# Modulation vectors as columns and a scaled transposing product in the opening stage of a hybrid attention and DeltaNet layer

## The chip, the cores and the metric

The kernel runs on one core of one Trainium2 chip. The core has five engines with queues of their own: TensorE (PE, with its weight loads shown apart as PEld), VectorE (DVE), ScalarE (ACT), GpSimd (POOL) and SyncE (SP, which here issues the loads). The metric is the device time of one execution in microseconds. The median of three runs of the kernel before is 1299.49 us (1299.34 to 1300.92).

## What is computed

One layer of a diffusion backbone over 512 latent tokens and 256 context tokens, with 1024 channels, in float32. Cut to what matters here:

```python
mod_lat = jax.nn.silu(c) @ w_mod + b_mod          # 1024 -> 6 x 1024
mod_ctx = jax.nn.silu(c_ctx) @ w_mod + b_mod
sh1, sc1, g1, sh2, sc2, g2 = split(mod_lat, 6)
hx = rms_norm(x)   * (1 + sc1)  + sh1             # latent rows
hc = rms_norm(ctx) * (1 + csc1) + csh1            # context rows
...                                               # hx, hc @ w_in, attention, gated DeltaNet, merge
x = x + g1 * merged
x = x + g2 * conv_ffn(rms_norm(x) * (1 + sc2) + sh2)
return rms_norm(x, final_norm_w)
```

The opening stage computes the first two of the six vectors for both `c` and `c_ctx` (2048 columns of `w_mod`), the RMS norms, and `hx` and `hc`, transposed so that channels lie on the 128 partitions. The other four vectors are made later, beside other work.

## The kernel before

The text below calls by their letters the steps that the string `ORD` lists. PE's instructions are kept in the order of that list (`pinned`, L548); on the other engines a scheduler orders instructions by priority and by its own estimate of time.

- **Loads** (`LORD`, L422 to L455): SP issues `x0 x1 x2` (the context rows and two halves of the latent rows, 1 MB each, tiles `xs`), `w0` to `w7` (eight chunks of `w_mod`, 1 MB each, tiles `wm`, `WB` = 3 buffers), and `h0 h1` (the first two weight tiles of the projections, `wraw`, 2 buffers), kept in this order. Then come the rope tables `tabs` and `wrow`.
- **d**: 16 products on zeros at the start (`warm`, L551).
- **Row norms** (L464 to L470): ACT squares each 128-row tile and sums the squares, DVE and POOL (the power of -0.5) make the factor `rs`, DVE multiplies the rows `xs` by it.
- **x** (`x_cols`, L507): four transposes of 128x128 of the scaled rows into one of two banks `pt`, copied out by DVE (even steps) or ACT (odd steps).
- **g** (`gemv`, L474): one of four blocks of 512 modulation columns. The moving operand is the chunk of `w_mod`, 512 wide, and the stationary one the columns of silu(c) and silu(c_ctx). For the first 4 or 6 of the 8 row blocks k (`FKS`) the weights are split into a rounded part `wmh` (ACT) and a rest `wml` (DVE or POOL, `GN`), both float32r, and `cs4` holds the split vectors; the other k go as plain float32. The result `pm` is a row, copied to `mrow` by DVE.
- **m** (`mod_cols`, L494): four small transposes of `mrow` into columns, and four additions on DVE.
- **y** (`modulate`, L519): for one pair of channel blocks, scale and shift (latent rows on DVE, context rows on POOL), then the split into a rounded part (ACT, `hxH`, `hcH`) and a rest (DVE, `hxL`, `hcL`).
- **p** (`early_proj`, L538): the products of one channel block with the two first weight tiles (`hw`), 12 matmuls, into the banks `pc` and `mb`. p0 and p1 need y0, p2 and p3 need y1, and so on.

After the opening follow the projections of keys, values and queries (tile `pq`, weights `w_aq`), whose matmuls are also kept in program order, with the other modulation vectors woven in (tiles `wmd`, `macc`).

Of the kernel before, what the change touches and what calls it, by code (L numbers as in the profile page):

```python
# [14 lines left out]
P = 128  # L15
D = 1024
# [19 lines left out]
KV = 10  # L36
GN = '023'
FKS = '4466'
ORD = 'd4 x0 x1 x2 x3 x4 x5 x6 x7 g0 x8 x9 x10 x11 m0 y0 g1 m1 y1 p0 g2 p1 m2 y2 p2 g3 p3 m3 p4 y3 p5 p6 p7'
RK = 1.0  # L40
# [3 lines left out]
TG = 1  # L44
WHB = 3
PMB = 1
XV, YV = 0, 2
NS = 2
# [6 lines left out]
LPIN = 1  # L55
LORD = 'x0 x1 x2 w0 w1 w2 w3 h0 h1 w4 w5 w6 w7'
WB = 3
P0 = 1
# [20 lines left out]
def hybrid_layer_body(tc, x, ctxt, xT, consts, cols, rows, w_mod1, w_mod2, w_db, w_aq, w_cm, w_pa, w_pd, w_out,  # L79
                      w_up, w_down, outT, dbg=None):  # L80
    nc = tc.nc
    V, A, G, SP = nc.vector, nc.scalar, nc.gpsimd, nc.sync
    pinned = [False]

# [22 lines left out]
    def tt(out, a, b, op, eng=None):  # L107
        (eng or V).tensor_tensor(out=out, in0=a, in1=b, op=op)  # L108

    def ts(out, a, s1, op0, s2=None, op1=None, eng=None):  # L110
        if op1 is None:
            (eng or V).tensor_scalar(out=out, in0=a, scalar1=s1, scalar2=None, op0=op0)
        else:
            (eng or V).tensor_scalar(out=out, in0=a, scalar1=s1, scalar2=s2, op0=op0, op1=op1)  # L114

# [3 lines left out]
    def act(out, a, f=AF.Copy, **kw):  # L119
        A.activation(out, a, f, **kw)  # L120

# [12 lines left out]
    with es:  # L134
# [7 lines left out]
        def first():  # L142
            return tc.high_priority(offset=2000000)
# [276 lines left out]
        with m1_es:  # L420
# [5 lines left out]
            def ordered_load(out, in_):  # L426
                i = SP.dma_start(out, in_)
                if LPIN:
                    tc.keep_in_program_order(i)

            hw = []
            for op in LORD.split():
                i = int(op[1])
                with sooner():
                    if op[0] == "w":
                        wms.append(m1.tile([P, 4, 512], F32, name="wm", tag="wm", bufs=WB))
                        ordered_load(wms[i], w_mod1[i // 2, i % 2])
                    elif op[0] == "h":
                        h, part = order[i]
                        raw = ws.tile([P, 1024], F32, name="wraw", tag="wraw", bufs=2)  # L440
                        ordered_load(raw, w_cm[8 * part + h])
                    elif i == 0:
                        ordered_load(xs[0], ctxt)
                    else:
                        ordered_load(xs[i], x[:, 2 * i - 2:2 * i, :])
                if op[0] == "h":
                    with first():
                        hi, lo = (m1.tile([P, 1024], F32R, name=n, tag=n, bufs=NS) for n in ("whi", "wlo"))
                        split(hi, lo, raw)
                        hw.append((hi, lo))  # L450
            with sooner():
# [7 lines left out]
            V.tensor_copy(csl, cs.rearrange("p (k two) -> p k two", two=2)[:, :, 0])  # L459
            cs4 = m1.tile([P, KT, 4], F32R, name="cs4")  # L460
            split(cs4[:, :, 0:2], cs4[:, :, 2:4], cs.rearrange("p (k two) -> p k two", two=2))
            ss = m1.tile([P, 6], F32, name="ss")
            rs = m1.tile([P, 6], F32, name="rs")
            for i in range(3):  # L464
                for t in range(2):
                    act(hxH[:, 6:8, :].rearrange("p a b -> p (a b)"), xs[i][:, t, :], AF.Square, accum_out=ss[:, 2 * i + t:2 * i + t + 1])
                sl = slice(2 * i, 2 * i + 2)
                rsqrt(rs[:, sl], ss[:, sl], 1.0 / D, EPS)
                for t in range(2):
                    ts(xs[i][:, t, :], xs[i][:, t, :], rs[:, 2 * i + t:2 * i + t + 1], ALU.mult)  # L470
            m2 = lambda t, o: t[:, o:o + 16].rearrange("p (s k) -> p s k", s=2)
            wsl = lambda k: slice(k * P, k * P + P)

            def gemv(nb, k0=0, k1=KT):  # L474
                if k0 == 0:
                    mpm[nb] = mps.tile([P, 512], F32, name="pm", tag="pm", bufs=PMB)[0:4]
                ps = mpm[nb]
                for k in range(k0, k1):
                    wm, j = wms[2 * nb + k // 4], k % 2
                    if k >= int(FKS[nb]):  # L480
                        mm(ps[0:2], cs[:, 2 * k:2 * k + 2], wm[:, k % 4, :], False, k == KT - 1)
                        continue
                    if j == 0:
                        wmh = m1.tile([P, 2, 512], F32R, name="wmh", tag="wmh", bufs=WHB)
                        wml = m1.tile([P, 2, 512], F32R, name="wml", tag="wml", bufs=WHB)
                        act(wmh, wm[:, k % 4:k % 4 + 2, :])
                        tt(wml, wm[:, k % 4:k % 4 + 2, :], wmh, ALU.subtract, G if k % 4 == 0 and str(nb) in GN else V)
                    mm(ps, cs4[:, k, :], wmh[:, j, :], k == 0, False)
                    mm(ps[0:2], cs4[:, k, 0:2], wml[:, j, :], False, k == KT - 1)
                if k1 == KT:  # L490
                    mrows[nb] = m1.tile([4, 512], F32, name="mrow", tag="mrow", bufs=2)
                    V.tensor_copy(mrows[nb], ps)

            def mod_cols(nb, mrow):  # L494
                pst = xbank()[:, 0, 0:16].rearrange("p (a b) -> p a b", b=4)
                for i in range(4):
                    T.transpose(pst[:, i, :], mrow[:, i * P:(i + 1) * P], ident[0:4, 0:4])
                ks = slice(2 * nb, 2 * nb + 2)
                p4 = pst.rearrange("p (s k) r -> p s k r", s=2)
                for j, md in enumerate((mod, modc)):  # L500
                    tt(m2(md, 0)[:, :, ks], p4[:, :, :, j], m2(col, S_BMOD)[:, :, ks], ALU.add)
                    tt(m2(md, 0)[:, :, ks], p4[:, :, :, 2 + j], m2(md, 0)[:, :, ks], ALU.add)

# [3 lines left out]
            def x_cols(j):  # L507
                i, kp = j // 4, j % 4
                dst = stash[1][kp] if i == 0 else stash[0][kp][:, :, 256 * i - 256:256 * i]
                pt = mps.tile([P, 2, 256], F32, name="pt", tag="pt", bufs=NB - PMB - NS)  # L510
                for a in range(2):
                    for t in range(2):
                        transpose(pt[:, a, t * P:(t + 1) * P], xs[i][:, t, wsl(2 * kp + a)])
                if j % 2 or j < XV:
                    act(dst, pt)
                else:
                    V.tensor_copy(dst, pt)

            def modulate(kp):  # L519
                for (hh, hl, md, pair), st in zip(sides, stash):  # L520
                    n = hh.shape[2]
                    hfs = []
                    for a in range(2):
                        k = 2 * kp + a
                        hf = m1.tile([P, n], F32, name="hf", tag="hf%d" % n, bufs=HB)
                        if n == NL or YV:
                            ts(hf, st[kp][:, a, :], md[:, 8 + k:9 + k], ALU.mult, md[:, k:k + 1], ALU.add,
                               G if YV == 2 and n < NL else V)
                        else:
                            act(hf, st[kp][:, a, :], AF.Identity, scale=md[:, 8 + k:9 + k], bias=md[:, k:k + 1])  # L530
                        hfs.append(hf)
# [14 lines left out]
            pinned[0] = True  # L546
            mrows, mpm = {}, {}
            wz = hxH[:, 5, :]  # L548
            V.memset(wz.bitcast(F32), 0.0)
# [7 lines left out]
            def step(what, i):  # L557
                if what == "g":
                    with sooner():
                        gemv(i)  # L560
                elif what in "ab":
                    with sooner():
                        gemv(i, 0 if what == "a" else 4, 4 if what == "a" else KT)
                elif what == "m":
                    with sooner():
                        mod_cols(i, mrows[i])
                elif what == "d":
                    with sooner():
                        warm(i)
                elif what == "x":  # L570
                    with sooner():
                        x_cols(i)
                elif what == "y":
                    with first():
                        modulate(i)
                else:
                    early_proj(i)

            for op in ORD.split():
                step(op[0], int(op[1:]))  # L580
            pinned[0] = False
            for (h, part), (ps, pc) in zip(order[:NS], hps):
# [91 lines left out]
        with kv_es:  # L674
# [30 lines left out]
            for blk in range(6):  # L705
                w2 = [load_w(w_aq[blk, i]) for i in range(2)]
                for t in range(6 if blk < 2 else 4):
# [878 lines left out]
```

## Time and profile before

| | us |
|---|---|
| median of 3 runs | 1299.49 |
| the profiled execution | 1298.72 |
| its span, first to last instruction | 1296.9 |
| PE busy in the span | 1219.5 |
| DVE busy | 847.1 |
| ACT busy | 625.4 |
| POOL busy | 308.1 |
| mean granted PE clock | 0.982 |

How such lines are read. In a timeline a line is: start, duration, engine, source line, operation, output<-inputs (moving operand, then stationary one), shapes, count, and in brackets the idle time before it with what ended it. In a row of windows it is: the window, its length, then busy time and count for PE, PEld, DVE, ACT and POOL, then the granted PE clock (1.00 is full speed), the share of the DMA engines and GB/s. In the view of waits it is: who <- for whom: total us, times, longest. A plain float32 product counts as two matmul records, a float32r product or a transpose as one. Matmuls overlap at their ends, so that the time from start to start is their pace.

### The profile page before, as it was taken

The page shows a single profiled execution, that of the slowest core. Times are in us where ns is not written, and L with a number is a line of the kernel's source. Part 1 is how long each engine was busy: PE and PEld are TensorE (multiplying, and loading weights), DVE is VectorE, ACT ScalarE, POOL GpSimd, SP SyncE. Part 2 cuts the span into 40 slices and gives each one's busy share as a digit, 9 for nine tenths or more (in the row PEclk, how much of TensorE's full clock was granted, in tenths as well). Part 3 has the DMA queues.
Part 4 walks back from the last instruction along what each step waited for, and adds up shares of the span by engine and source line. Part 5 has one row for each costly group of instructions (what it writes and reads, how often), then busy time and mean ns, then how long its engine had stood idle before and what let it go on. Part 6 is the DMA issues. An engine that isn't in the chain of part 4 may idle for free.

```text
span 1296.9 us, 20854 instructions
## 1 busy us (share of the span) xinstructions
PE 1219.5 (94%) x7835; PEld 1026.6 (79%) x7835; DVE 847.1 (65%) x1625; ACT 625.4 (48%) x1403; POOL 308.1 (24%) x364
## 2 busy tenths in 40 slices
PE   7899999999988899889998999899999999999997
PEld 3487878999877778778787878688988888888886
DVE  5886977777779876775655556555676666663323
ACT  5454656666576665573443533233354444443221
POOL 1753420000123459659455400000000000000000
PEclk9999999999999999999998999899999999999998
DMA  8656731121353642533633654365042323333331
GB/s 318 228 170 203 232 111 62 66 86 46 108 180 135 190 140 86 185 121 116 192 126 105 179 173 137 99 221 184 9 130 98 98 98 98 97 94 89 92 99 66
DMA packets 70790, 170.82 MB, mean 132 GB/s; under 512 B 7872, under 2 KB 18720, under 8 KB 69280
## 3 DMA queue, kind: packets, MB, share of 16 engines
q1 hardware_dynamic: 70688, 169.47, 39.9%
q8 instruction: 62, 1.02, 0.3%
q14 instruction: 40, 0.33, 0.1%
HBM read 144.23 MB, written 25.21 MB: 131 GB/s over the span
## 4 chain that ended last, share of the span: by engine, by line
PE 64%; DVE 11%; POOL 10%; DMA 5%; issue 3%; ACT 2%; SPq 0%; POOLq 0%; DVEq 0%; ACTq 0%
PE mc L87 32%; PE mb L87 17%; POOL R L108 4%; POOL prod L108 4%; PE pb L87 4%; PE pS L87 3%; PE ab L87 2%; PE pq L87 2%; DMA Gb<-gamdr 2%; PE ab L91 1%; DVE wlo L108 1%; PE pk L87 1%; PE xb L91 1%; DMA wmd<-in_w_mod_dram 1%; DVE macc L377 1%
## 5 line engine op out<-in xcount | busy, mean ns | idle before, releaser
L108 DVE TENSOR_TENSOR wlo<-wraw,whi 128x1024 fp32r<-128x1024 f32 x152 | 189.8, 1250 | 161.0 <-ACT whi L120 159.1
L120 ACT ACTIVATE whi<-wraw 128x1024 fp32r<-128x1024 f32 x152 | 159.0, 1048 | 200.0 <-PE mc L87 104.5
L87 PE MATMUL mc<-h,whi 128*128 128x512 f32 (+1 forms) x752 | 219.7, 376 | 0.3 <-ACT whi L120 0.3
L87 PE MATMUL mb<-hxH,whi 128*128 128x512 f32 x384 | 162.6, 424 | 2.3 <-DVE R L108 2.1
L87 PEld LDWEIGHTS mc<-h,whi 128*128 128x128 f32 x752 | 138.0, 188 | 25.9 <-ACT whi L120 0.5
L87 PE MATMUL mb<-hxH,wlo 128*128 128x512 f32 x384 | 152.6, 397 | 0.0
L87 PE MATMUL mb<-hxL,whi 128*128 128x512 f32 x384 | 152.0, 396 | 0.0
L87 PE MATMUL mc<-h,wlo 128*128 128x512 f32 (+1 forms) x376 | 141.3, 376 | 0.5 <-DVE wlo L108 0.5
L108 POOL TENSOR_TENSOR rc<-rc,mhalf 128x2 f32<-128x2 f32 x4 | 3.0, 740 | 460.0 <-DVE rc L114 460.0
L87 PE MATMUL mc<-a,whi 128*128 128x512 f32 (+1 forms) x396 | 111.4, 367 | 0.6 <-DVE x L117 0.6
L87 PEld LDWEIGHTS mb<-hxH,wlo 128*128 128x128 f32 x384 | 73.0, 190 | 16.7
L87 PEld LDWEIGHTS mb<-hxH,whi 128*128 128x128 f32 x384 | 73.7, 192 | 13.3 <-ACT t L120 2.3
L87 PEld LDWEIGHTS mc<-a,whi 128*128 128x128 f32 x396 | 71.3, 188 | 13.1 <-DVE x L117 0.8
L87 PEld LDWEIGHTS mc<-h,wlo 128*128 128x128 f32 x376 | 70.8, 188 | 13.8 <-DVE wlo L108 1.0
L87 PEld LDWEIGHTS mb<-hxL,whi 128*128 128x128 f32 x384 | 73.8, 192 | 9.7
L87 PE MATMUL mc<-a,wlo 128*128 128x512 f32 (+1 forms) x198 | 72.7, 367 | 0.0
L117 DVE SCALAR_TENSOR_TENSOR u<-mc,col,u 128x511 f32<-128x511 f32 x88 | 65.4, 747 | 1.4
L108 POOL TENSOR_TENSOR prod<-X,R 128x31 f32<-128x31 f32 (+15 forms) x93 | 54.5, 586 | 21.6 <-DVE X L108 14.7
L108 POOL TENSOR_TENSOR R<-R,prod 128x31 f32<-128x31 f32 (+15 forms) x93 | 55.9, 601 | 6.8
L87 PE MATMUL pq<-whi,hxH 128*128 128x256 f32 x192 | 55.3, 288 | 0.0
L87 PE MATMUL pq<-wlo,hxH 128*128 128x256 f32 x192 | 53.5, 279 | 0.2 <-DVE wlo L108 0.2
L87 PE MATMUL pq<-whi,hxL 128*128 128x256 f32 x192 | 53.3, 278 | 0.0
(348 smaller groups left out, 2876.7 us busy)
## 6 DMA issues: line engine op xcount, KB each, us to landing
wraw<-in_w_cm_dram SPq DMA_DIRECT2D x48, 512.0 KB, 4.2
wraw<-in_w_up_dram SPq DMA_DIRECT2D x44, 512.0 KB, 3.7
wmd<-in_w_mod_dram SPq DMA_DIRECT2D x64, 256.0 KB, 3.7
wm<-in_w_mod_dram SPq DMA_DIRECT2D x8, 1024.0 KB, 8.3
wraw<-in_w_down_dram SPq DMA_DIRECT2D x16, 512.0 KB, 3.6
wraw<-in_w_aq_dram SPq DMA_DIRECT2D x12, 512.0 KB, 4.7
M<-gamdr SPq DMA_DIRECT2D x64, 64.0 KB, 4.8
wraw<-in_w_pa_dram SPq DMA_DIRECT2D x8, 512.0 KB, 4.4
```

The lines of the kernel that those rows point to most:

```text
L87: i = nc.tensor.matmul(*a, **k)
L91: i = nc.tensor.transpose(*a, **k)
L108: (eng or V).tensor_tensor(out=out, in0=a, in1=b, op=op)
L117: V.scalar_tensor_tensor(out=out, in0=a, scalar=s, in1=b, op0=op0, op1=op1)
L120: A.activation(out, a, f, **kw)
L377: held(V.scalar_tensor_tensor(out=av, in0=wk, scalar=csl[:, k:k + 1], in1=av, op0=ALU.mult, op1=ALU.add))
```

## The change

The four blocks of the vectors come out as columns at once: the chunk of `w_mod` becomes the stationary operand, in slices of 128x128, and the two columns of silu(c) and silu(c_ctx) the moving one, all in plain float32. The splits, the row copies and the small transposes go. `g` becomes two steps, `a` and `b`, one for each half of the 8 row blocks, and all four blocks write into one bank `pms`. The row factor is no longer multiplied into `xs`: DVE writes it onto a diagonal `dg` (new step `g`, `diagonals`), and the transposing product multiplies with that diagonal. The squares (step `s`) are shared by ACT and DVE. Context rows are scaled and shifted by ACT (`YV` is gone). `put` keeps DVE's and ACT's instructions of this stage in program order. `WB` is 6, `h0 h1` load earlier, and the first block of `w_aq` (`q0 q1`) is loaded and split as part of the stage.

```diff
-GN = '023'
-FKS = '4466'
-ORD = 'd4 x0 x1 x2 x3 x4 x5 x6 x7 g0 x8 x9 x10 x11 m0 y0 g1 m1 y1 p0 g2 p1 m2 y2 p2 g3 p3 m3 p4 y3 p5 p6 p7'
+ORD = 'd4 s0 s1 g0 x0 x1 g1 x2 x3 s2 x4 x5 g2 x6 x7 a0 x8 x9 x10 x11 b0 m0 y0 h0 h1 a1 b1 m1 y1 p0 p1 a2 b2 m2 y2 p2 a3 b3 m3 y3 q0 q1 p3 p4 p5 p6 p7'
...
-LORD = 'x0 x1 x2 w0 w1 w2 w3 h0 h1 w4 w5 w6 w7'
-WB = 3
+LORD = 'x0 x1 x2 w0 w1 h0 h1 w2 w3 w4 w5 w6 w7 q0 q1'
+WB = 6
...
+    def put(i):
+        return tc.keep_in_program_order(i) if ordered[0] else i
...
-        (eng or V).tensor_tensor(out=out, in0=a, in1=b, op=op)
+        put((eng or V).tensor_tensor(out=out, in0=a, in1=b, op=op))
...
-        A.activation(out, a, f, **kw)
+        put(A.activation(out, a, f, **kw))
...
-            cs4 = m1.tile([P, KT, 4], F32R, name="cs4")
-            split(cs4[:, :, 0:2], cs4[:, :, 2:4], cs.rearrange("p (k two) -> p k two", two=2))
...
-            for i in range(3):
-                for t in range(2):
-                    act(hxH[:, 6:8, :].rearrange("p a b -> p (a b)"), xs[i][:, t, :], AF.Square, accum_out=ss[:, 2 * i + t:2 * i + t + 1])
-                sl = slice(2 * i, 2 * i + 2)
-                rsqrt(rs[:, sl], ss[:, sl], 1.0 / D, EPS)
-                for t in range(2):
-                    ts(xs[i][:, t, :], xs[i][:, t, :], rs[:, 2 * i + t:2 * i + t + 1], ALU.mult)
+            dg = m1.tile([P, 6, P], F32, name="dg")
+            def squares(i):
+                for t, o in ((0, 4), (1, 6)):
+                    sq, xi = hxH[:, o:o + 2, :].rearrange("p a b -> p (a b)"), xs[i][:, t, :]
+                    acc = ss[:, 2 * i + t:2 * i + t + 1]
+                    if t == 0:
+                        act(sq, xi, AF.Square, accum_out=acc)
+                    else:
+                        put(V.scalar_tensor_tensor(out=sq, in0=xi, scalar=1.0, in1=xi, op0=ALU.mult, op1=ALU.mult, accum_out=acc))
+                rsqrt(rs[:, 2 * i:2 * i + 2], ss[:, 2 * i:2 * i + 2], 1.0 / D, EPS)
+
+            def diagonals(i):
+                for t in range(2 * i, 2 * i + 2):
+                    ts(dg[:, t, :], ident, rs[:, t:t + 1], ALU.mult)
...
+            def weights(op):
+                if op[0] == "h":
+                    hi, lo = (m1.tile([P, 1024], F32R, name=n, tag=n, bufs=NS) for n in ("whi", "wlo"))
+                else:
+                    hi, lo = (ws.tile([P, 1024], F32R, name=n, tag=n, bufs=3) for n in ("whi", "wlo"))
+                split(hi, lo, raws[op])
+                (hw if op[0] == "h" else qw).append((hi, lo))
...
-                    mm(ps, cs4[:, k, :], wmh[:, j, :], k == 0, False)
-                    mm(ps[0:2], cs4[:, k, 0:2], wml[:, j, :], False, k == KT - 1)
...
+            pms = mps.tile([P, 4, 2, 2, 2], F32, name="pm", tag="pm", bufs=PMB)
+
+            def gemv(nb, half):
+                for k in range(4):
+                    wm, kc = wms[2 * nb + half], 4 * half + k
+                    for i in range(4):
+                        mm(pms[:, nb, i // 2, i % 2, :], wm[:, k, wsl(i)], cs[:, 2 * kc:2 * kc + 2],
+                           kc == 0 and i == 0, kc == KT - 1 and i == 3)
+
+            def mod_cols(nb):
                 ks = slice(2 * nb, 2 * nb + 2)
-                p4 = pst.rearrange("p (s k) r -> p s k r", s=2)
                 for j, md in enumerate((mod, modc)):
-                    tt(m2(md, 0)[:, :, ks], p4[:, :, :, j], m2(col, S_BMOD)[:, :, ks], ALU.add)
-                    tt(m2(md, 0)[:, :, ks], p4[:, :, :, 2 + j], m2(md, 0)[:, :, ks], ALU.add)
+                    tt(m2(md, 0)[:, :, ks], pms[:, nb, :, :, j], m2(col, S_BMOD)[:, :, ks], ALU.add)
...
-                        transpose(pt[:, a, t * P:(t + 1) * P], xs[i][:, t, wsl(2 * kp + a)])
+                        mm(pt[:, a, t * P:(t + 1) * P], xs[i][:, t, wsl(2 * kp + a)], dg[:, 2 * i + t, :])
...
-                w2 = [load_w(w_aq[blk, i]) for i in range(2)]
+                w2 = qw if blk == 0 else [load_w(w_aq[blk, i]) for i in range(2)]
```

More of the change, by code (lines that the diff above doesn't have):

```diff
@@ L44 @@
 TG = 1
-WHB = 3
 PMB = 1
-XV, YV = 0, 2
+XV = 0
 NS = 2
@@ L82, in hybrid_layer_body @@
     V, A, G, SP = nc.vector, nc.scalar, nc.gpsimd, nc.sync
-    pinned = [False]
+    pinned, ordered = [False], [False]
+    def put(i):
+        return tc.keep_in_program_order(i) if ordered[0] else i
     class Ordered:
@@ L107, in tt @@
     def tt(out, a, b, op, eng=None):
-        (eng or V).tensor_tensor(out=out, in0=a, in1=b, op=op)
+        put((eng or V).tensor_tensor(out=out, in0=a, in1=b, op=op))
     def ts(out, a, s1, op0, s2=None, op1=None, eng=None):
         if op1 is None:
-            (eng or V).tensor_scalar(out=out, in0=a, scalar1=s1, scalar2=None, op0=op0)
+            put((eng or V).tensor_scalar(out=out, in0=a, scalar1=s1, scalar2=None, op0=op0))
         else:
-            (eng or V).tensor_scalar(out=out, in0=a, scalar1=s1, scalar2=s2, op0=op0, op1=op1)
+            put((eng or V).tensor_scalar(out=out, in0=a, scalar1=s1, scalar2=s2, op0=op0, op1=op1))
     def stt(out, a, s, b, op0, op1):
@@ L429, in ordered_load @@
                     tc.keep_in_program_order(i)
-            hw = []
+            raws, qw = {}, []
             for op in LORD.split():
@@ L437, in hybrid_layer_body @@
                         ordered_load(wms[i], w_mod1[i // 2, i % 2])
-                    elif op[0] == "h":
+                    elif op[0] in "hq":
                         h, part = order[i]
-                        raw = ws.tile([P, 1024], F32, name="wraw", tag="wraw", bufs=2)
-                        ordered_load(raw, w_cm[8 * part + h])
+                        raws[op] = ws.tile([P, 1024], F32, name="wraw", tag="wraw", bufs=2)
+                        ordered_load(raws[op], w_cm[8 * part + h] if op[0] == "h" else w_aq[0, i])
                     elif i == 0:
@@ L445, in hybrid_layer_body @@
                         ordered_load(xs[i], x[:, 2 * i - 2:2 * i, :])
[L446 to L450, printed above, removed]
             with sooner():
@@ new lines, in diagonals @@
+            def diagonals(i):
+                for t in range(2 * i, 2 * i + 2):
+                    ts(dg[:, t, :], ident, rs[:, t:t + 1], ALU.mult)
+            hw = []
+            def weights(op):
[5 more added lines that the diff above has]
+                (hw if op[0] == "h" else qw).append((hi, lo))
@@ L471, in hybrid_layer_body @@
             m2 = lambda t, o: t[:, o:o + 16].rearrange("p (s k) -> p s k", s=2)
             wsl = lambda k: slice(k * P, k * P + P)
[L474 to L487, printed above, removed]
-                    mm(ps, cs4[:, k, :], wmh[:, j, :], k == 0, False)
-                    mm(ps[0:2], cs4[:, k, 0:2], wml[:, j, :], False, k == KT - 1)
-                if k1 == KT:
-                    mrows[nb] = m1.tile([4, 512], F32, name="mrow", tag="mrow", bufs=2)
-                    V.tensor_copy(mrows[nb], ps)
@@ L494, in mod_cols @@
[L494 to L497, printed above, removed]
+            pms = mps.tile([P, 4, 2, 2, 2], F32, name="pm", tag="pm", bufs=PMB)
[5 more added lines that the diff above has]
+                           kc == 0 and i == 0, kc == KT - 1 and i == 3)
@@ L516, in x_cols @@
                 else:
-                    V.tensor_copy(dst, pt)
+                    put(V.tensor_copy(dst, pt))
             def modulate(kp):
@@ L525, in modulate @@
                         hf = m1.tile([P, n], F32, name="hf", tag="hf%d" % n, bufs=HB)
-                        if n == NL or YV:
-                            ts(hf, st[kp][:, a, :], md[:, 8 + k:9 + k], ALU.mult, md[:, k:k + 1], ALU.add,
-                               G if YV == 2 and n < NL else V)
+                        if n == NL:
+                            ts(hf, st[kp][:, a, :], md[:, 8 + k:9 + k], ALU.mult, md[:, k:k + 1], ALU.add)
                         else:
@@ L546, in hybrid_layer_body @@
             pinned[0] = True
-            mrows, mpm = {}, {}
-            wz = hxH[:, 5, :]
+            wz = hxH[:, 3, :]
             V.memset(wz.bitcast(F32), 0.0)
@@ L557, in step @@
             def step(what, i):
[L558 to L576, printed above, removed]
+                with first() if what == "y" else sooner():
+                    if what in "ab":
+                        gemv(i, int(what == "b"))
+                    elif what in "hq":
+                        weights(what + str(i))
+                    elif what != "p":
+                        {"s": squares, "g": diagonals, "m": mod_cols, "d": warm, "x": x_cols, "y": modulate}[what](i)
+                if what == "p":
                     early_proj(i)
+            ordered[0] = True
             for op in ORD.split():
                 step(op[0], int(op[1:]))
-            pinned[0] = False
+            pinned[0] = ordered[0] = False
             for (h, part), (ps, pc) in zip(order[:NS], hps):
```

## The prediction

> **What bounds the kernel now.** First the page's busy shares: one engine carries the span.
>
> ```profile
> PE 1219.5 (94%) x7835; PEld 1026.6 (79%) x7835; DVE 847.1 (65%) x1625; ACT 625.4 (48%) x1403; POOL 308.1 (24%) x364
> ```
>
> TensorE (PE) is idle for 1296.9 - 1219.5 = 77 us of the whole span. Next the timeline of PE, for where the opening begins and ends, and the same stretch by windows, with the one after it (the key and query projections, tile pq).
>
> ```profile
> 11.03 0.33 PE L91 MATMUL pt<-cst,xs 128*128 128x128 f32 x1 [3.98 <-DVE xs L112]
> ...
> 70.48 0.28 PE L87 MATMUL pq<-whi,hcH 128*128 128x256 f32 x1
> ```
>
> ```profile
> 11.03:70.48 59.45, 48.61 (x225) 26.84 (x225) 47.04 (x70) 29.84 (x46) 33.47 (x19) 0.97 0.66 244
> 70.48:182.47 111.99, 106.00 (x822) 92.48 (x820) 96.65 (x255) 61.83 (x179) 44.12 (x34) 1.00 0.61 199
> ```
>
> The opening runs on PE from 11.03 to 70.48, 59.45 us, of which PE works 48.61 and idles 10.84. After it PE is 95% busy and runs its matmuls in a fixed order, so a shift of 70.48 reaches the end nearly whole. Half of what ends the idle time, in the view of the waits, is work that the change removes:
>
> ```profile
> PE xb L91 <- DVE mrow L492: 4.1, 3, 2.0
> PE pm L87 <- POOL wml L108: 2.1, 3, 1.0
> ```
>
> So the prize is at most 10.84 us, and only if PE's own work does not grow.
>
> **The change part by part.** *The vectors (a, b, m).* Before, a chunk of w_mod streams past 2 or 4 stationary columns; split products take about 0.24 us each, unsplit ones two records of 0.43.
>
> ```profile
> 29.42 0.39 PE L87 MATMUL pm<-wmh,cs 128*4 128x512 f32 x1
> ...
> 31.37 3.60 PE L87 MATMUL pm<-wm,cs 128*2 128x512 f32 x8
> ```
>
> By the code 40 split products (8+8+12+12) and 12 unsplit ones: 40 x (31.37 - 29.42)/8 + 24 x 0.43 = 9.8 + 10.3 = 20.1 us. After, the chunks are stationary: 4 blocks x 2 halves x 4 k x 4 slices = 128 unsplit products with 2 moving columns. The tail of the kernel has the same shape, stationary 128x128 with one moving column:
>
> ```profile
> 912.44 0.36 PE L87 MATMUL mc<-cst,sq 128*128 128x1 f32 x2
> ...
> 913.11 0.48 PE L87 MATMUL mc<-y,whi 128*128 128x256 f32 x2
> ```
>
> Three such products, of two records each, lie between 912.44 and 913.11: 0.223 us each, far more than one column needs, so the weight load sets the pace. 128 x 0.223 = 28.5 us, so PE gains 8.4 us of work here, 3.57 us a half. It loses the transposes of mrow, 4 x 0.4 us, and the 6.2 us of waits above:
>
> ```profile
> 60.46 0.41 PE L91 MATMUL xb<-cst,mrow 4*128 4x4 f32 x4 [0.65 <-DVE mrow L492]
> ```
>
> DVE, ACT and POOL lose the splits, which only PE waited for.
>
> *The transposing product (g, x).* 48 transposes become full products with a diagonal; a full 128x128 product of the kernel:
>
> ```profile
> 16.79 1.09 PE L91 MATMUL pt<-cst,xs 128*128 128x128 f32 x8 [0.88 <-ACT hcL L120]
> ```
>
> ```profile
> 538.52 1.95 PE L87 MATMUL pb<-dl,M 128*128 128x128 f32 x16
> 540.40 0.21 PE L87 MATMUL pb<-o_tr,NN 32*32 32x32 f32 x1
> ```
>
> 0.11 us a transpose before; (540.40 - 538.52)/8 = 0.235 or less a product after, taken as the 0.223 above: 48 x 0.223 = 10.7 against 5.2, so +5.5 us.
>
> *The start.* In DVE's new order the first diagonal stands behind the square of the second tile, and that waits for its load:
>
> ```profile
> 9.38 1.06 ACT L120 ACTIVATE hxH<-xs 128x1024 fp32r<-128x1024 f32 x1 [0.17 <-DMA xs<-in_x_dram]
> ```
>
> ```profile
> L112 DVE TENSOR_SCALAR dg<-cst,rc x8: 279/284/288, 914.3 to 1289.1; 128x128 f32<-128x128 f32 x8
> ```
>
> 9.38, an estimated 1.2 for a 1024-wide pass on DVE (1.06 is ACT's), its row factor, two diagonals of 0.28 that overlap: about 11.2, where it stood at 11.03.
>
> *Fixed order: waits it adds.* x4's copy stands on DVE behind the third square's row factor, which waits for ACT, which does x3's copy first; PE has two banks and waits some 1.0 us at x6. All gemv results share one bank, so a1 waits for m0, 0.7 us by the 0.65 of the row above; a2 and a3 have p0, p1, p2 between. The last modulation, y3, took this long before, with POOL in its chain:
>
> ```profile
> 60.91 0.16 DVE L108 TENSOR_TENSOR mod<-xb,col 128x4 f32<-128x4 f32 x1 [0.50 <-PE xb L91]
> ...
> 64.71 2.92 DVE L108 TENSOR_TENSOR hcL<-hf,hcH 128x256 fp32r<-128x256 f32 x2 [0.84 <-POOL hf L114]
> ```
>
> At most 67.6 - 60.9 = 6.7 us, now with ACT in POOL's place: cost nothing, hidden beside p3, p4, p5 (6.4 us, next); without that cover p6 would wait for all of it. The q splits lie beside p6 and p7.
>
> *Early projections.* The same 16 groups, 1.06 us each:
>
> ```profile
> 63.02 0.28 PE L87 MATMUL pc<-hcH,whi 128*128 128x256 f32 x1
> ...
> 64.08 0.28 PE L87 MATMUL pc<-hcH,whi 128*128 128x256 f32 x1
> ```
>
> 17.0 us. *Loads.* Before, the fourth w_mod load waits for a buffer, the last two later still:
>
> ```profile
> 21.98 0.33 SPq L427 DMA_DIRECT2D wm<-in_w_mod_dram  x1
> 34.99 5.80 SPq L427 DMA_DIRECT2D wm<-in_w_mod_dram  x2
> ```
>
> With 6 buffers six go out at once, the last two wait for a0 and b0 (near 25 and 33) and are wanted at a3, after 50; behind them in SP's queue stand q0, q1, which wait for the h splits near 39, then the tables, wanted at pq. All hidden, cost nothing; a load would have to take over 17 us (50 less 33) to hold a3.
>
> **Sum with the clock as it is.** 11.2 + 10.7 + 28.5 + 17.0 + 1.0 + 0.7, plus 1.7 for the half-clock window after the idle start (below; it is there before too) = 70.8. Against 70.48: +0.3 us. The prize is spent on weight loads.
>
> **The clock.** The windows are 3.41 us apart:
>
> ```profile
> 8.39:11.80 3.41, 0.43 (x2) 0.24 (x3) 1.65 (x4) 3.12 (x6) 0.70 (x1) 1.00 1.01 425
> 11.80:15.21 3.41, 3.41 (x15) 2.72 (x15) 2.72 (x5) 1.75 (x4) 0.70 (x1) 0.50 1.01 428
> 15.21:18.63 3.42, 1.78 (x13) 1.27 (x12) 2.13 (x4) 3.42 (x6) 1.57 (x2) 1.00 0.98 409
> 18.63:22.04 3.41, 2.05 (x10) 0.81 (x11) 3.41 (x3) 2.66 (x4) 1.60 (x1) 1.00 0.12 44
> 390.68:394.09 3.41, 1.32 (x9) 1.06 (x8) 3.41 (x6) 2.00 (x5) 1.85 (x1) 1.00 0.10 32
> 394.09:397.51 3.42, 3.42 (x10) 2.64 (x10) 3.32 (x9) 1.36 (x3) 1.35 (x1) 0.50 0.73 214
> 1284.97:1288.39 3.42, 1.91 (x17) 1.74 (x15) 0.65 (x2) 0.42 (x1) 0.26 (x1) 1.00 0.63 223
> 1288.39:1291.80 3.41, 1.19 (x4) 0.93 (x4) 1.76 (x6) 0.00 (x0) 0.44 (x1) 0.50 0.01 2
> ```
>
> The second column is PE's busy time, the third from last the granted clock. After a window with 0.43 or 1.32 us the clock is half in the next; after 1.78 (15.21) it stays whole (18.63). It came back after windows full of work (11.80). One window breaks this: 1284.97 has 1.91, yet 1288.39 is at 0.50. What it holds:
>
> ```profile
> 1285.77 0.28 PE L87 MATMUL mc<-cst,acc 128*128 128x1 f32 x2
> 1286.96 0.38 PE L87 MATMUL mc<-cst,sq 128*128 128x1 f32 x2 [0.91 <-ACT sq L120]
> ```
>
> Up to 1285.77 it streams (0.80 us); the rest is idle time and one-column products behind full weight loads, that of 1286.96 and two pairs more. Counted, the window looks like 15.21, which kept the clock; not counted, like those that lost it. So such products count for little, and the 128 new ones are of that kind. What half clock does to full loads:
>
> ```profile
> 531.14 2.08 PE L87 MATMUL pb<-r,TTm 128*128 128x128 f32 x8 [4.21 <-DVE r L117]
> 532.87 0.77 PE L87 MATMUL mb<-hxH,whi 128*128 128x512 f32 x1
> ```
>
> 1.73 us for 8 records, 0.216 instead of 0.11. So, with a fall on average a window and a half (5.1 us) into a stretch of these products: b0 to b1 lasts 10.7, of which 5.6 run at half (+5.6); p0 and p1 run half for some 2.6 us' worth before a full window brings the clock back (+2.6); a2, b2: 7.1 - 5.1 = 2.0 (+2.0); p2 is too short for a full window (+2.1); a3, b3 all at half (+7.1); p3 on (+2.6). Together +22. The bounds: nothing, if the clock holds, and 45.5 (28.5 + 17.0), if all of them and all early projections run at half; 22 lies between, since the full windows of p0, p1 and of p3 on must bring the clock back as at 15.21.
>
> The Trainium skill, TensorE: Matmul & The Clock Gate, Part 1, gives such a window of 3413 ns and ties the clock to how busy PE was; the trace agrees with the period (11.80, 15.21). It does not say whether a weight load counts as busy; if it does, the page's rule gives the first rival.
>
> **The rivals.** (1) *The clock holds* in these stretches, since half-counted loads would do: one window is thin evidence, and any weight between none and about half fits it. The sum above: 1298.72 + 0.3 = 1299.0, give or take 2.5 for the next stage's order. (2) *The clock falls, but loads keep their pace*, only x and p pay: x8 to x11 1.7, p 2.6 + 2.1 + 2.1 = +8.5: 1307.5. Against it stand the 0.216 above, which could be the 128 moving columns rather than the load. The Trainium skill, same page, section LDWEIGHTS, prices a load by its columns alone and gives no second figure for the low clock; that is this rival, and no run here shows a load alone at half clock. (3) *Faster: the next stage fills its holes.* PE idles 111.99 - 106.00 = 6.0 us there, DVE is 86% busy. If the clock holds and the early-split q weights and the idle POOL (33.47 us busy in the opening before) take those holes out: 1299.0 - 6.0 = 1293. It decides from the point where the wlo of the second weight block is there before PE asks. Against it: DVE's work in that stage is unchanged. (4) *The change doesn't take effect*: the scheduler could keep the old overlap; but orders are pinned, so it has no chance of its own.
>
> **How the numbers follow.** Profiled execution 1298.72 (span 1296.9, 1.8 around it), 0.77 below the median 1299.49. Forecast: 1298.72 + 0.3 + 22 = 1321.0, chance 0.52, own range 1315 to 1326 (where in a window a stretch begins). Rival 1: 0.28; rival 2: 0.10; rival 3: 0.10. Range 1296 to 1326: it leaves out rival 3 and the forecast's top. Measurement tells about 0.2% (2.6 us) from no change: faster 0.10 + 0.04 of rival 1 = 0.14; same 0.17 of rival 1; slower 0.52 + 0.10 + 0.07 = 0.69.
>
> **What would show it.** Products pm<-cs with 128x2 moving, paced 0.11 us a record warm and 0.22 at half; a granted clock of 0.50 in windows from about 32 to 50 and again before 75; pq starting near 93. If the clock stays 1.00 past the first idle, pq starts near 71 and rival 1 holds. A pace under 0.10, or PE waiting on DMA wm, would break the sum itself.

## The result, and the profile after

| | before | after |
|---|---|---|
| median, us | 1299.41 (4 runs, 1295.41 to 1300.92) | 1317.31 (4 runs, 1314.84 to 1322.35) |
| ratio | | 1.015, 95% interval 1.0127 to 1.0174 |
| profiled execution | 1298.72 | 1318.86 |
| its span | 1296.9 | 1316.8 |
| mean granted PE clock | 0.982 | 0.967 |
| first pq product (the end of the opening) | 70.48 | 89.66 |
| first pq to first score product (pS) | 113.2 | 117.3 |

The changed kernel is 1.5% slower. First the busy line of the page after:

```profile
PE 1251.0 (95%) x8059; PEld 1076.7 (82%) x8059; DVE 832.3 (63%) x1613; ACT 615.8 (47%) x1394; POOL 282.0 (21%) x351
```

DVE, ACT and POOL do less than before, as the change says. PE is busy 31.5 us longer, for 224 more records. The timeline of PE over the opening says where:

```profile
11.33 8.59 PE L87 MATMUL pt<-dg,xs 128*128 128x128 f32 x48 [3.26 <-DVE dg L112]
20.60 2.05 PE L87 MATMUL pt<-dg,xs 128*128 128x128 f32 x16 [0.67 <-DVE hxL L512]
22.48 3.63 PE L87 MATMUL pm<-cs,wm 128*128 128x2 f32 x32
25.98 3.97 PE L87 MATMUL pt<-dg,xs 128*128 128x128 f32 x32
29.79 3.63 PE L87 MATMUL pm<-cs,wm 128*128 128x2 f32 x32
33.74 13.12 PE L87 MATMUL pm<-cs,wm 128*128 128x2 f32 x64 [0.32 <-DVE modc L108]
46.72 0.56 PE L87 MATMUL pc<-hcH,whi 128*128 128x256 f32 x1
...
53.21 8.90 PE L87 MATMUL pm<-cs,wm 128*128 128x2 f32 x64
61.97 0.56 PE L87 MATMUL pc<-hcH,whi 128*128 128x256 f32 x1
...
65.64 10.88 PE L87 MATMUL pm<-cs,wm 128*128 128x2 f32 x64
76.38 0.56 PE L87 MATMUL pc<-hcH,whi 128*128 128x256 f32 x1
...
89.66 0.28 PE L87 MATMUL pq<-whi,hcH 128*128 128x256 f32 x1
```

32 records of two columns take 3.50 us in a0 (22.48 to 25.98), 0.109 each; 64 of them take 12.98 in a1 b1, 8.76 in a2 b2 and 10.74 in a3 b3. Inside these stretches nothing waits: the same instructions run at another pace. The windows of the changed kernel (3.41 us each; the second column is PE's busy time, the third from last the granted clock):

```profile
31.12:34.53 3.41, 3.09 (x28) 3.00 (x28) 1.07 (x4) 0.29 (x1) 0.00 (x0) 1.00 0.28 82
34.53:37.95 3.42, 3.42 (x18) 3.42 (x18) 2.18 (x5) 3.42 (x8) 0.00 (x0) 0.50 0.70 292
...
48.19:51.60 3.41, 3.41 (x12) 2.93 (x12) 2.05 (x4) 2.24 (x6) 0.00 (x0) 0.50 0.00 0
51.60:55.01 3.41, 3.41 (x26) 3.15 (x26) 0.00 (x0) 0.00 (x0) 0.00 (x0) 1.00 0.00 0
55.01:58.43 3.42, 3.42 (x33) 3.42 (x32) 0.00 (x0) 0.00 (x0) 0.00 (x0) 1.00 0.00 0
58.43:61.84 3.41, 3.41 (x18) 3.41 (x17) 0.00 (x0) 0.00 (x0) 0.00 (x0) 0.50 0.00 0
61.84:65.25 3.41, 3.41 (x13) 3.02 (x13) 2.50 (x6) 2.33 (x5) 0.00 (x0) 0.50 0.03 7
65.25:68.67 3.42, 3.42 (x31) 3.33 (x30) 0.76 (x2) 0.42 (x2) 0.00 (x0) 1.00 0.00 0
68.67:72.08 3.41, 3.41 (x18) 3.41 (x18) 0.00 (x0) 0.00 (x0) 0.00 (x0) 0.50 0.00 0
```

The reader is to see two things. The clock falls at 34.53, at 58.43 and at 68.67, each after a window in which PE shows 3.09 or 3.42 us of work, all or (in the last) nearly all of it two-column products. And it comes back at 51.60 and at 65.25, each after a window filled with the wide products of p0 p1 or p2. In between it stays at half, from 34.53 to 51.60, although PE is busy without a gap. A record takes 0.214 us there ((46.72 - 34.53) / 57, the records that are left after 34.53 at 0.11 each): the load itself is twice as slow at half clock.

Behind the opening, a second loss. Three views of the changed kernel (PE, ACT, and SP's queue), and SP's queue before:

```profile
102.14 0.36 PE L87 MATMUL pq<-whi,hxH 128*128 128x256 f32 x1 [3.76 <-DVE qt L117]
```

```profile
98.57 0.21 ACT L120 ACTIVATE rowt<-rowt 128x16 f32<-128x16 f32 x1 [3.97 <-DMA rowt<-in_rows_dram]
```

```profile
82.83 5.85 SPq L202 DMA_DIRECT2D wraw<-in_w_aq_dram  x3
88.78 3.13 SPq L375 DMA_DIRECT2D wmd<-in_w_mod_dram  x5
91.95 0.43 SPq L581 DMA_DIRECT2D rowt<-in_rows_dram  x1
```

```profile
58.93 2.41 SPq L375 DMA_DIRECT2D wmd<-in_w_mod_dram  x5
61.39 0.43 SPq L598 DMA_DIRECT2D rowt<-in_rows_dram  x1
```

Before, rowt's load is issued 9.1 us ahead of the first pq product (61.39 against 70.48); after, 2.3 us behind it (91.95 against 89.66). ACT waits 3.97 us for it, DVE's rows stand behind that, and PE, whose order is fixed, idles 3.76 us. The wait also costs clock: the window from 99.39 to 102.80 holds 0.67 us of PE's work, and the next one, to 106.21, runs at 0.50. From the first pq to the first pS it takes 117.3 instead of 113.2 us. Later something comes back, and nothing of the change lies there: windows over the stretch from the last key product of DeltaNet to the first merge product, before and then after:

```profile
653.50:873.20 219.70, 205.25 (x1382) 172.84 (x1382) 124.30 (x251) 83.67 (x185) 51.33 (x80) 0.96 0.46 148
```

```profile
678.50:893.50 215.00, 203.12 (x1383) 171.16 (x1382) 125.25 (x251) 83.56 (x186) 51.85 (x80) 0.98 0.46 151
```

215.0 against 219.7 us for the same work, at a clock of 0.98 instead of 0.96; the stretch ahead of it goes the other way (278.7 after at 0.96, 276.7 before at 0.98). The grid of the windows does not start with the kernel (the first falls, at 11.80 before and at 10.64 after, lie 1.2 us apart on it), so which gaps cost a half-clock window can differ from execution to execution. Some of the runs' spread of 7 us may come from there; that is not shown. In the profiled executions the opening is thus 19.2 us longer (89.66 against 70.48), the way to pS 4.1 longer, and the rest 3.4 shorter: together the 19.9 us of the two spans.

### The profile page after: what moved, and what is told of

Read it like the earlier page. It is cut to its first block, busy times and chain, and to the rows that moved or that the text cites. A ratio compares the mean times of both kernels' runs of the same rounds, so it can differ in the third digit from the quotient of the medians.

```text
span 1316.8 us, 21242 instructions
## 1 busy us (share of the span) xinstructions
PE 1251.0 (95%) x8059; PEld 1076.7 (82%) x8059; DVE 832.3 (63%) x1613; ACT 615.8 (47%) x1394; POOL 282.0 (21%) x351
## 4 chain that ended last, share of the span: by engine, by line
PE 67%; DVE 11%; POOL 8%; DMA 5%; ACT 4%; issue 3%; SPq 0%; DVEq 0%; POOLq 0%; ACTq 0%
PE mc L87 31%; PE mb L87 16%; PE pq L87 4%; POOL R L108 4%; POOL prod L108 3%; PE pb L87 3%; PE pm L87 3%; PE pS L87 3%; PE ab L87 2%; DVE wlo L108 2%; PE ab L91 1%; PE pt L87 1%; DMA wmd<-in_w_mod_dram 1%; DMA Gb<-gamdr 1%; PE xb L91 1%
## 5 line engine op out<-in xcount | busy, mean ns | idle before, releaser
L87 PE MATMUL mb<-hxH,whi 128*128 128x512 f32 x384 | 165.5, 431 | 3.3 <-DVE R L108 2.1
L87 PEld LDWEIGHTS mc<-h,wlo 128*128 128x128 f32 x376 | 70.8, 188 | 13.6 <-DVE wlo L108 1.0
```

What stands on the lines that cost most here:

```text
L87: i = nc.tensor.matmul(*a, **k)
```

## The experiments

The theory: the clock follows the time in which columns stream through PE; the time in which weights load counts for nothing or little. The rivals: that something else in the new code lowers it (a1's wait, the fixed order, plain float32), and, for the second loss, that DVE's own work is late rather than SP's queue. All kernels start from the changed one. Results (medians of 4 to 12 runs), each ratio against the kernel before on the same chip; its median was 1296.6 to 1299.4 us on the four chips, so that kernels are best compared by their ratios. The last two columns are of the profiled execution, in us:

| run | median, us | ratio (95% interval) | first pq | first pq to pS |
|---|---|---|---|---|
| 32 columns | 1313.78 | 1.0112 (1.0082 to 1.0143) | 88.0 | 116.7 |
| 64 columns | 1298.96 | 1.000 (0.9978 to 1.0021) | 70.4 | 116.1 |
| 128 columns | 1299.53 | 1.0015 (0.9996 to 1.0035) | 70.7 | 117.3 |
| 128, scaled rows | 1294.42 | 0.9963 (0.9944 to 0.9982) | 66.8 | 116.5 |
| 64, early q splits | 1294.30 | 0.9973 (0.9955 to 0.9990) | 71.6 | 114.5 |
| 64, free order | 1292.24 | 0.9945 (0.9924 to 0.9965) | 68.2 | 113.0 |
| 64, scaled, early q splits | 1293.91 | 0.9959 (0.9941 to 0.9978) | 66.7 | 114.6 |
| blocks 2, 3 as rows | 1300.86 | 1.0016 (1.0002 to 1.0030) | 73.6 | 115.1 |
| changed kernel, free order | 1314.49 | 1.0135 (1.0102 to 1.0168) | 92.7 | 113.6 |
| 64, scaled, free order | 1297.57 | 1.0006 (0.9990 to 1.0021) | 72.1 | 114.7 |
| rows, free order | 1306.33 | 1.0069 (1.0046 to 1.0092) | 78.0 | 116.5 |
| 128, scaled, free order | 1296.19 | 0.9980 (0.9965 to 0.9995) | 69.2 | 115.3 |

**More columns behind the same loads** (`MW` = 32, 64, 128). The two columns of silu are repeated, by a stride of zero; the sums that are used are the same. The wider result no longer fits four blocks into one bank, so each block has a tile of its own, one after the other in that bank; this is alike in all three kernels, and only `MW` tells them apart.

```diff
-                        mm(pms[:, nb, i // 2, i % 2, :], wm[:, k, wsl(i)], cs[:, 2 * kc:2 * kc + 2],
+                        mm(pms[nb][:, i // 2, i % 2, :].rearrange("p (r two) -> p r two", two=2), wm[:, k, wsl(i)],
+                           cs[:, 2 * kc:2 * kc + 2].unsqueeze(1).to_broadcast([P, MW // 2, 2]),
```

> The moving operand of the 128 vector products is repeated from 2 to 32 columns; the 256 weight loads stay as they are. Theory 'streaming counts': the granted clock follows the time in which columns stream, not the time in which weights load. 32 columns stream some 0.027 of each 0.11 us record, a quarter, 0.85 us of a 3.41 us window: less than the 1.3 us that lost the clock before, so it falls again, windows at 0.50 in a1 b1 and a3 b3, total 1315 to 1323. Rival 'something else' (a wait, the plain float32 products, the length of the work): the same, 1315 to 1323. This run tells the two apart only together with 128.

> As with 32, but 64 columns: they stream half of each record, 1.7 us of a window, near the 1.78 us that kept the clock before. 'Streaming counts': the clock holds at 1.00 from the end of x on, pq starts near 71 to 74, total 1298 to 1304. 'Something else': 1315 to 1323, windows at 0.50 as in the changed kernel.

> 128 columns: streaming fills each record as in the diagonal products, for 64 times the useful work. 'Streaming counts': no window at 0.50 after the first one, pace of a0 to b3 0.11 us a record throughout, pq starts near 71 to 73, total 1298 to 1304 although PE multiplies more. 'Something else': 1315 to 1323 or more.

PE's timelines, 32 columns, then 64, then 128:

```profile
32.10 13.32 PE L88 MATMUL pm<-cs,wm 128*128 128x32 f32 x64 [0.37 <-PE pm L88]
```

```profile
32.09 7.33 PE L88 MATMUL pm<-cs,wm 128*128 128x64 f32 x64 [0.37 <-PE pm L88]
```

```profile
20.93 3.74 PE L88 MATMUL pm<-cs,wm 128*128 128x128 f32 x32
24.50 3.89 PE L88 MATMUL pt<-dg,xs 128*128 128x128 f32 x32
...
32.33 7.38 PE L88 MATMUL pm<-cs,wm 128*128 128x128 f32 x64 [0.37 <-PE pm L88]
...
43.76 7.31 PE L88 MATMUL pm<-cs,wm 128*128 128x128 f32 x64
50.82 0.36 PE L88 MATMUL pc<-hcH,whi 128*128 128x256 f32 x1
...
53.01 7.30 PE L88 MATMUL pm<-cs,wm 128*128 128x128 f32 x64
60.08 0.37 PE L88 MATMUL pc<-hcH,whi 128*128 128x256 f32 x1
...
70.67 0.28 PE L88 MATMUL pq<-whi,hcH 128*128 128x256 f32 x1
```

Sixty-four times the columns cost next to nothing at full clock (3.57 us for a0 against 3.50) and take 18 us off the whole. Between 32 and 64 columns the same waits, orders and loads go from 13.3 to 7.3 us in a1 b1. The rival is out: what decides is how long columns stream in a window. Before, a record of 512 columns took 0.43 us, which is 0.027 for 32 columns and 0.054 for 64; in records of 0.109 us that is an estimated 0.85 us of streaming in a window of 3.41 with 32 columns, and 1.7 with 64. The totals came as expected but for 32 columns, 1.2 us under their range.

**The diagonal undone**, on top of 128 columns.

```diff
-                for t in range(2 * i, 2 * i + 2):
-                    ts(dg[:, t, :], ident, rs[:, t:t + 1], ALU.mult)
+                for t in range(2):
+                    ts(xs[i][:, t, :], xs[i][:, t, :], rs[:, 2 * i + t:2 * i + t + 1], ALU.mult)
...
-                        mm(pt[:, a, t * P:(t + 1) * P], xs[i][:, t, wsl(2 * kp + a)], dg[:, 2 * i + t, :])
+                        transpose(pt[:, a, t * P:(t + 1) * P], xs[i][:, t, wsl(2 * kp + a)])
```

> On top of 128 columns, the rows are scaled by the factor as before and the x steps are plain transposes again, one record each. By the prediction's term the diagonal costs 48 x (0.223 - 0.11) = 5.5 us: 5 us less than with 128 columns alone if x is bound by PE, 1293 to 1299. If x is bound by the copies out of the banks or by the scaling of the rows on DVE (six passes that stand ahead of x), little or nothing is gained: within 2 us of 128 columns.

5.1 us less in the medians; 3.8 of it in the profiled opening (66.8 against 70.7). Of the 5.5 that the work is worth there, 1.0 goes to longer waits of PE beside x (1.6 us in four places instead of 0.6) and 0.35 to a later start. The total is as expected; both kernels lose one window of x to half clock, near 12 to 16.

**Early q splits, and the order left free**, on top of 64 columns.

```diff
-... m1 y1 p0 p1 a2 b2 m2 y2 p2 a3 b3 m3 y3 q0 q1 p3 ...
+... m1 y1 q0 q1 p0 p1 a2 b2 m2 y2 p2 a3 b3 m3 y3 p3 ...
```

> With 64 columns, and the splits of the first two query-and-key weight tiles (q0, q1) moved in the fixed order from behind y3 to behind y1. Theory 'SP queue': these splits free the two buffers that the next weight loads wait for, and behind those stand in SP's queue the loads of the late vectors, of rowt and of dbraw, which come 8 us later than before the change; that is the idle time of PE after the opening (2.1 us at 81, 1.0 at 91) that before does not have. Then SP issues them near 47 instead of 66 to 74, the idle time goes, first pq to first pS is 113 to 114 us instead of 116.1, total 2 to 4 us below 64 columns alone. Rival 'order of VectorE': the idle time comes from what DVE and ACT do after the opening, and stays: within 1 us.

```diff
-            ordered[0] = True
             for op in ORD.split():
```

> With 64 columns, and VectorE's and ScalarE's instructions of the stage left to the scheduler (only TensorE's and SP's orders are kept). The prediction put the cost of the fixed order at about 1.0 us (PE waits 0.6 us at x6). If that is all, the opening ends 0 to 1 us earlier. The scheduler also puts a third split of a weight tile before y2, which by 'SP queue' brings the loads behind it forward: total 1 to 4 us below 64 columns. If the fixed order earned something, the opening ends later than 70.4.

PE's start with the free order:

```profile
9.17 3.99 PE L88 MATMUL pt<-dg,xs 128*128 128x128 f32 x32 [1.92 <-DVE dg L113]
```

SP's queue with 64 columns, then with early splits:

```profile
66.35 1.46 SPq L203 DMA_DIRECT2D wraw<-in_w_aq_dram  x2
...
73.18 0.43 SPq L585 DMA_DIRECT2D rowt<-in_rows_dram  x1
```

```profile
46.41 6.03 SPq L203 DMA_DIRECT2D wraw<-in_w_aq_dram  x3
...
71.57 0.33 SPq L585 DMA_DIRECT2D rowt<-in_rows_dram  x1
```

And PE's waits from 34 to 112 with 64 columns (whom it waits for: total us, times, longest), then those with early splits:

```profile
PE pq L88 <- DVE qt L118: 2.1, 1, 2.1
PE pq L88 <- DVE wlo L109: 1.2, 1, 1.2
```

```profile
PE pq L88 <- DVE wlo L109: 2.3, 1, 2.3
```

With early splits SP issues the next weight loads 20 us earlier (46.4 instead of 66.4) and the wait for qt is gone, but the one for the second block's wlo is 1.1 us longer; the way to pS falls from 116.1 to 114.5, not to the 113 to 114 that were expected. The loads behind did not come near 47 either: rowt's is issued 1.6 us earlier than with 64 columns alone (2.8 by its distance from pq), because SP now waits for it until PE's last early projection is done (8.3 us on PE's mb). So the late splits held the queue, and once they are out of the way the next wait in it shows. The ratio falls by 0.0027, some 3.5 us, though the two intervals overlap and the two profiled executions lie the other way round (1299.70 against 1294.93). The free order gives more, and more than the 1 to 4 us that were expected: the first transposing product starts at 9.17 instead of 10.86, as DVE's first diagonals no longer stand behind its square of the first latent rows, and no window of x loses the clock in this execution (1.00 from 9.17 to 29.83), so the opening ends 2.2 us earlier; the way to pS is 113.0. This is the fastest kernel of the study: 0.9945 of before, 7 us. The fixed order cost time, some five of the seven microseconds in these two places.

**The findings together.**

> 64 columns, rows scaled and transposed as before the change, q0 q1 split early: the three findings together, if they add. 1299 less 5 (the diagonal) less 3 (SP queue): 1289 to 1293. If the key stage is bound by something else, 1293 to 1296.

They do not add: 0.9959, against 0.9963 for scaled rows with 128 columns. In the profiled executions the end of the opening is the same (66.7, 66.8), the way to pS is 1.9 us shorter and the whole 5.5 us shorter (1290.89 against 1296.44), but the runs spread over 10 us and their medians lie 0.5 us apart. Why the medians show nothing of it is open.

**Blocks 2 and 3 as rows**, split, to save PE's work (new step c: ACT writes the rounded half of two row blocks, DVE or POOL the rest). It stands on top of 64 columns for blocks 0 and 1, scaled rows and early q splits, whose rests POOL writes; there are 4 buffers for the chunks instead of 6.

```diff
+                act(hi, wm[:, k:k + 2, :])
+                tt(lo, wm[:, k:k + 2, :], hi, ALU.subtract, G if q in POOLC else V)
...
+                    mm(pms[nb], cs4[:, k, :], hi[:, k % 2, :], k == 0, False)
+                    mm(pms[nb][0:2], cs4[:, k, 0:2], lo[:, k % 2, :], False, k == KT - 1)
```

> A try to beat both: on top of the scaled rows, blocks 0 and 1 of the vectors as columns with 64 moving columns, blocks 2 and 3 as rows again with split weights (0.47 us a row block by the 0.235 us of each split product, instead of 0.89), the splits on ScalarE and VectorE, three of eight rests on GpSimd, whose rows show 2.8 us each, q0 q1 split early with their rests on GpSimd. PE's work falls by 16 x 0.42 = 6.7 us less the small transposes 0.8. If DVE and ACT keep up, the opening ends near 61 and the total is 1283 to 1288; if PE waits for the splits (2.8 us on GpSimd, or the second block's weights with 4 buffers), it gains nothing over the kernel without rows: 1290 to 1294.

A miss. PE waits for a split, and DVE is held up while POOL writes a rest (PE, DVE and POOL of this kernel):

```profile
58.61 0.59 PE L92 MATMUL pm<-wmh,cs 128*4 128x512 f32 x1 [4.34 <-ACT wmh L125]
```

```profile
52.25 3.04 DVE L119 TENSOR_SCALAR hf<-hxL,mod 128x512 f32<-128x512 f32 x2
```

```profile
51.20 3.35 POOL L113 TENSOR_TENSOR wlo<-wraw,whi 128x1024 fp32r<-128x1024 f32 x1
```

DVE's two passes take 3.04 us beside POOL's 3.35; in the 64-column kernel, with POOL idle, they take 1.00. It is the first of the two that is long: 2.58 us, to 54.83, just behind the end of POOL's pass at 54.55; the second takes 0.54. ACT stands behind DVE, and PE idles 4.34 us, with the clock at half on both sides of it (0.59 a product instead of 0.39).

**The order free on other kernels.**

> The changed kernel itself, 2 moving columns, with VectorE's and ScalarE's order left to the scheduler. Clock and order are separate terms: the clock still falls in a1 b1 and a3 b3 (about 19 us), the order gives back what it gave with 64 columns (1299.0 - 1292.2 = 6.7 us), total 1309 to 1313. If the fixed order had brought the clock down (through the wait of a1 or the start), the total comes near 1292.

> 64 columns, rows scaled and transposed as before the change, order left to the scheduler: of the change only the vectors as columns (widened), the early loads and the shared squares are left. If the terms add, 1292.2 - 5 = 1286 to 1289, the opening ends near 63. If the scaling of the rows on DVE stands ahead of the first transpose again, the opening gains only 3: 1288 to 1291.

> The try with blocks 2 and 3 as split rows once more, all rests on DVE (none on GpSimd) and the order left to the scheduler, the products of p2 and p3 set between the halves to give the splits time. If what held the first try was GpSimd (2.8 us a rest, and DVE's two passes of 1.0 us took 3.0 beside it) and the fixed order, PE waits little: 1281 to 1288. If the splits themselves are what PE waits for, 1290 to 1298.

In the last of these DVE writes all the rests, and the products of p2 and p3 stand between the halves of blocks 2 and 3. The first agrees in kind and not in size: the clock falls all the same, so the fixed order has no part in it; the way to pS is 113.6 instead of 117.3, which fits SP's queue, though the free order moves more than the q splits, and the other kernels of this group took 114.7 to 116.5; but the opening ends later (92.7): x starts earlier, the windows lie elsewhere, and two-column products bring the clock down at 20.2 (within a0) and 30.5, where with the fixed order they first did at 34.5. In total the free order gives nothing clear here (1.0135 against 1.015, each inside the other's interval). The other two miss their ranges by 6.6 and 8.3 us. Windows of the 64-column kernel with scaled rows:

```profile
12.78:16.20 3.42, 1.53 (x13) 1.12 (x11) 2.69 (x6) 0.96 (x3) 1.81 (x2) 1.00 1.00 422
16.20:19.61 3.41, 2.71 (x14) 1.98 (x11) 3.25 (x5) 1.76 (x3) 0.04 (x1) 0.50 1.03 418
19.61:23.03 3.42, 3.42 (x18) 3.42 (x17) 1.85 (x2) 1.44 (x2) 0.00 (x0) 0.50 1.01 422
23.03:26.44 3.41, 3.41 (x18) 3.41 (x18) 0.00 (x0) 0.00 (x0) 0.00 (x0) 0.50 1.01 418
26.44:29.85 3.41, 3.41 (x17) 3.04 (x16) 1.38 (x2) 0.62 (x2) 0.00 (x0) 0.50 1.03 412
29.85:33.27 3.42, 3.42 (x32) 3.41 (x31) 0.00 (x0) 0.58 (x1) 0.00 (x0) 1.00 0.50 207
```

The plain transposes are half as long as the products with the diagonal, and with their waits they leave 1.53 us of work in a window: the clock falls, and stays down for all of a0, whose 64 columns fill half of each record. It comes back only after a window of transposes. The diagonal's extra time had kept the clock up; the other executions agree, with a mean granted clock of 0.973 to 0.981 in all twelve, against 0.984 to 0.989 in the six with the diagonal (64, free order). The rows kernel falls into the same hole (0.50 from 12.2 to 29.3), and again in a1 (36.1 to 49.8). One run tells whether the width of a0 decides it:

> The kernel with scaled rows and free order missed: its clock fell at 16.2, after a window with 1.53 us of transposes, and did not come back during a0, though PE was busy 3.42 of 3.42 us there (64 columns). Only the width changes here, 64 to 128. Theory 'streaming counts, and to come back a window must be nearly full of it': 64 columns fill half of a record, enough to keep the clock and not to raise it; 128 fill it, so the clock comes back in the window after the first that a0 fills, near 23 instead of 30, or does not fall: the opening ends 3 to 5 us earlier (67 to 69 instead of 72.1), total 1290 to 1295. Rival 'the clock comes back by itself after some windows, whatever PE does': back near 30 again, 1296 to 1300.

```profile
19.03:22.44 3.41, 3.41 (x18) 3.41 (x17) 2.81 (x3) 1.67 (x3) 0.00 (x0) 0.51 1.02 423
22.44:25.85 3.41, 3.06 (x28) 2.83 (x28) 0.72 (x2) 0.37 (x1) 0.00 (x0) 1.00 1.01 418
```

With 128 columns the first window that a0 fills brings the clock back, at 22.44; with 64 columns two such windows (19.61 and 23.03) did not, and it came back at 29.85. The opening ends 2.9 us earlier, at 69.2, although the clock fell earlier here, at 12.20. The total, 1296.19, is a little over the expected range and inside the rival's, and the two ratios' intervals just overlap (0.9980 and 1.0006), so it is the windows of these two executions and not the totals that speak against a clock that comes back by itself. So, in these traces, 64 columns hold a clock that is up and don't raise one that is down.

## Why the prediction was right, point by point

The forecast was 1321.0 with a range of its own from 1315 to 1326, and the median is 1317.31.

- **The sum at whole clock** (70.8): the kernel with 128 columns has the same work and order at whole clock but for one window, and its opening ends at 70.67. Term by term: start 11.2, measured 11.33 (11.05 there); the vectors 28.5, eight times 3.57 = 28.6; a wait of 1.0 at x6, measured 0.67; 0.7 at a1, measured 0.32. The prize was spent on weight loads, as the sum had it. A load with next to nothing behind it took twice as long at half clock: 0.214 us against 0.109. Rival 2 rested on the opposite. The Trainium skill, TensorE: Matmul & The Clock Gate, section LDWEIGHTS, has one figure for a load, by its columns alone.
- **The clock** (+22): right in kind, too high by some 3 (89.66 - 70.67 = 19.0). The changed kernel's timeline against that of 128 columns gives each term:

| stretch | predicted | measured |
|---|---|---|
| a1 b1 p0 p1 | 5.6 + 2.6 | (53.21 - 33.74) - (43.76 - 32.33) = 8.0 |
| a2 b2 | 2.0 | (61.97 - 53.21) - (50.82 - 43.76) = 1.7 |
| p2 | 2.1 | (65.64 - 61.97) - (53.01 - 50.82) = 1.5 |
| a3 b3 | 7.1 | (76.38 - 65.64) - (60.08 - 53.01) = 3.7 |
| p3 on | 2.6 | (89.66 - 76.38) - (70.67 - 60.08) = 2.7 |

The step that was mis-sized is "p2 is too short for a full window" and with it "a3, b3 all at half". At half clock p2 lasts 3.67 us (by the prediction's own terms it would be 2.1 + 2.1, more than a window), the window from 61.84 to 65.25 was nearly all p2, and the clock was whole again until 68.67. Against that, the start lost two half-clock windows and not one (10.64 to 17.47): x0 to x5 took 8.59 us, 7.41 with 128 columns.
- **The thin evidence held.** The one window at 1284.97 from which the prediction took that loads do not count is borne out by a1 b1, a2 b2 and a3 b3, with 2 columns and with 32. The Trainium skill, same page, Part 1, has the clock fall after an idle window and rise after a busy one. Read with loads as busy, the rule would have kept the clock after the window from 31.12 to 34.53 (3.09 us), and the trace disagrees. Read as streaming, it fits that window, but one need not be idle to lose the clock: the 1.53 us at 12.78 above did too.
- **Loads and q splits** ("all hidden, cost nothing"): wrong. The loads of q0 and q1 were hidden, but the step that counts is their splits' place at the end of the fixed order. It holds both buffers, and so the next weight loads and everything behind them in SP's queue. The way to pS grew by 4.1 us in the profiled execution, and the largest item in it is the 3.76 us that PE waits behind rowt; moving the splits alone, with 64 columns, gave back 1.6. The total did not show it: the opening was 3 us under the forecast, and the stretches from pS to the merge gave back some 3 in windows that fell better. That the total came so near to 1321.0 is in this part luck.
- **The start and the fixed order**: costed as a shift of 0.2 and 1.0 us of wait, which is about what it came to beside before (0.3 and 0.67). That the same code without the fixed order starts 1.7 us earlier was not seen.
- **The rivals.** Rival 1, the clock holds, is what 64 or 128 columns make of the kernel: 1299.0 by the prediction, 1298.96 and 1299.53 measured. Rival 3, the next stage fills its holes, did not come: up to pS it grew by 1 to 4 us in all kernels with the fixed order, and took 113.0 in the best, where it took 113.2 before.

## What to carry to other kernels

A product with few moving columns behind a full weight load costs the load, and in these runs it also counted as idle time for the clock: before moving work from the streaming to the stationary side, count the microseconds per 3.41 us window in which columns stream. If they are too few, more columns are free up to the load's own time. An order written out by hand must be read for what each engine's queue holds back, SP's too: the last instruction that frees a buffer sets when every later load is issued.

## What the runs showed of the hardware

- Windows by their start in the two kernels with scaled rows and free order: the clock was lost after a window with 1.53 us of transposes (12.78) and held with 64 columns (an estimated 1.7 us of streaming); where between them the limit lies was not measured. To rise it took a nearly full window: 2.71 (16.20) did not do, nor did 3.42 us of 64-column products (19.61); 3.41 us of 128-column ones (19.03) did.
- A shorter instruction can cost time through this: transposes in place of products twice as long took the clock down from 16.20 to 29.85.
- A pass of DVE over 128x512 that started while POOL ran a pass over 128x1024 took 2.58 us instead of 0.5 and ended 0.3 us behind POOL's; the next one took 0.54 again.
